# Stick-breaking attention with keys in rising order and factors applied after the value product; retention values projected 512 columns at a time

## The chip, the cores and the metric

The kernel runs on one core of one Trainium2 chip. TensorE is called PE here (its weight loads are PEld), VectorE is DVE, ScalarE is ACT, GpSimd is POOL, and SP issues most of the DMAs. The metric is the device time of one execution in microseconds (us); several runs of each kernel are compared by their median. About 0.2%, some 6 us, is what a measurement of this kernel can tell from no change.

## The reference, cut to what matters

Two layers of a decoder on 1024 tokens of width 1024. The change touches two places: the stick-breaking attention of layer 0 (8 heads of 64, causal without the diagonal), and the value projection of the retention of layer 1 (4 heads, 512 value columns each).

```python
def block(args):                                   # one block of 128 queries, all keys
    z = jnp.einsum('bhqd,bhkd->bhqk', q_i, k) * scale
    mask = kpos[None, :] < qpos[:, None]
    log_fail = jnp.where(mask, jax.nn.log_sigmoid(-z), 0.0)
    later = lax.cumsum(log_fail, axis=3, reverse=True) - log_fail
    a = jnp.where(mask, jnp.exp(jax.nn.log_sigmoid(z) + later), 0.0)
    return jnp.einsum('bhqk,bhkd->bhqd', a, v)
...
proj = h @ w_in                                    # retention: rq, rk, rv, rg are column ranges of proj
```

So the weight of key s for query t is exp(z_ts - softplus(z_ts) - the sum of softplus(z_tj) over the keys j between s and t).

## The kernel before, in words

Large products are made of float32r operands split into a high and a low part: three matmuls hi·hi, lo·hi, hi·lo per 128 rows of the contraction (`mm3`, L182 to L185). Weights come from HBM in units of 128x1024 by `w_pump`: SP loads `raw`, ACT casts `whi` (L168), DVE subtracts `wlo` (L169); three units at most are in flight.

**Stick-breaking (L849 to L1018)** works on scores laid out with keys on the partitions and queries along the free dimension. A *step* is one block of 128 keys against 256 queries of two heads, so its tiles are 128x512. There are 80 steps: 20 for each of four pairs of heads p, and within a pair two chains of query blocks are interleaved, i = 3 then 0 in one and i = 2 then 1 in the other. Query block i has 2i+2 key blocks. Of the 20 steps of a pair, 4 have kb = 2i+1, where only the last 128 queries of each head count (c0 = 128): these *diagonal* steps have 128x256 tiles, and the other 16 *full* steps have 128x512.

The engines run this part in the order in which the code is written (`manual_schedule`). In iteration n the loop goes through a list of tokens `SORDER`, each the stage of a step with an offset from n:

```python
SORDER = "Z+3 V-4 f Q+0 A+3 W+0 K+3 X-1 E+3 p p h+2 L+3 f C-1 l+2 M+3".split()
LSB, ABB, SHB = 8, 4, 3
```

The stages before: Z (PE, L869, L870, and a mask product L872 near the diagonal) writes z into a PSUM bank, of which pool `pz` has two; A, E, L (ACT, L877, L880, L883) make ln(1 + exp(-|z|)) in `ab`; K (DVE, L887) copies z to `ls` in SBUF; M (DVE, L890) makes softplus(z) from `ls` and `ab`; h (DVE, L896) and l (POOL, L899) split it into `sh` and `sl`; Q (PE, L910, L911) adds minus its sum over this block's own keys to a running PSUM bank `Pb` of the chain; W (DVE, L914) adds `Pb` to `ls`; X (ACT, L973) takes the exponential, the attention weight; C (PE, L922, L923) adds to `Pb` the rest of this block, for the next one (not in a chain's last step of a query block); V (PE, L932) multiplies by the values and sums all blocks of one query block in a PSUM bank `av`, which ACT copies to `ob` at the end (L934). The keys go down from the diagonal, so that `Pb` holds all later blocks. An f32 product like V stands in the trace as two instructions.

The token `f` (twice in an iteration) puts other PE work between: until n = 8 the last values' projection of layer 0 (`vps`, L464, four units of 3 matmuls of 256 columns an iteration), and from n = 18 on the first half of the output projection (`ops`, L183 to L185: 64 units of three 128x512 matmuls, spread at about one an iteration). An odd share goes to the first `f`, so a share of one leaves the second `f` empty. From n = 13 to 19 four tiles of `xs` are split there (L988 on ACT, L989 on DVE). The token `p` advances the preparation of the next pair's keys and queries (ACT L525 and L537, POOL L527 and L543), begun at the iterations that `PREPS` lists.

**Retention values (`v_half`, L1479 to L1500)**: for each head and each half of the tokens, 512 tokens times 512 columns with a contraction of 1024. Tokens are the stationary operand and the weights move, 256 columns at a time: 192 matmuls of 128x256, into `rvps`. It runs for heads 0 to 2 of the first half (while `norm_ops` makes the second half's inputs on DVE, ACT and POOL), then for heads 0 to 3 of the second half, and once more (head 3, first half) inside the retention core later.

Of the kernel before, what the change touches and what calls it, by code (L numbers as in the profile page):

```python
# [11 lines left out]
F32R = mybir.dt.float32r  # L12
AF = mybir.ActivationFunctionType
# [48 lines left out]
def tile_trunk(ctx: ExitStack, tc: tile.TileContext, xT, cbc, adaT, vec, w_hyb, w_hout, w_rin, w_rout,  # L62
# [443 lines left out]
    def stack(tag, nm, p, half):  # L506
        i = 2 * p + 1 - half
        return (sqs[0] if i % 3 else sb0).tile([P, HT], F32R, tag=tag, name=nm, bufs=2 if i % 3 else 1)

    def prep_qk(p, isq, half, new, dma=None):  # L510
# [3 lines left out]
        if not isq:  # L514
# [7 lines left out]
            for h in range(2):  # L522
                kh = stacks[p, "kh", h, half] = stack(f"kh{h}", f"kh{p}{h}", p, half)
                kl = stacks[p, "kl", h, half] = stack(f"kl{h}", f"kl{p}{h}", p, half)
                A.copy(kh, xs_[h])  # L525
                yield
                G.tensor_tensor(kl, xs_[h], kh.bitcast(F32), op=ALU.subtract)  # L527
                yield
# [5 lines left out]
        for h in range(2):  # L534
            o = slice(h * 64, h * 64 + 64)
            qs = stacks[p, "q", h, half] = stack(f"q{h}", f"q{p}{h}", p, half)
            A.copy(qs[o], x[o])  # L537
            ts.append(qs)
            yield
# [6 lines left out]
    def s_first():  # L546

        scr = sb0.tile([P, 4, P], F32R, tag="scr", name="scr")
        G.dma_start(scr[:, 0:3, :], cst[:, C_NSTR:C_NSTR + 3, :])
        V.tensor_copy(scr[:, 3, :], ident)  # L550
        scrs.append(scr)
        for isq in range(2):
            for _ in prep_qk(0, isq, 1, half_tile):
                pass
# [294 lines left out]
    with ExitStack() as sx:  # L849
        pz = sx.enter_context(tc.tile_pool(name="pz", bufs=2, space=PSUM))  # L850
        pP = sx.enter_context(tc.tile_pool(name="pP", bufs=1, space=PSUM))
        pav = sx.enter_context(tc.tile_pool(name="pav", bufs=1, space=PSUM))
        steps = []
        for p in range(4):
            two = [[dict(p=p, i=i, kb=kb, x=x, first=(kb == 2 * i + 1), last=(kb == 0), c0=128 if kb == 2 * i + 1 else 0)
                    for i in ii for kb in range(2 * i + 1, -1, -1)] for x, ii in enumerate(((3, 0), (2, 1)))]
            for pair in zip(*two):
                steps.extend(pair)
        cur = {}
        fin = []  # L860
# [13 lines left out]

        def stage_a(s):
            s["ab"] = ab = sp_.tile([P, HT], F32, tag="ab", name="ab", bufs=ABB).rearrange("p (h n) -> p h n", h=2)[:, :, s["c0"]:]
            A.activation(ab, s["z"], AF.Abs)  # L877
# [7 lines left out]
        def stage_k(s):  # L885
            s["ls"] = ls = sp_.tile([P, HT], F32, tag="ls", name="ls", bufs=LSB).rearrange("p (h n) -> p h n", h=2)[:, :, s["c0"]:]
            V.tensor_copy(ls, s["z"])  # L887

        def stage_sp(s):
            V.scalar_tensor_tensor(s["ab"], s["ls"], 0.0, s["ab"], op0=ALU.max, op1=ALU.add)  # L890

        def stage_hi(s):
            c0 = s["c0"]
            s["sh"] = sp_.tile([P, 2, 256], F32R, tag="sh", name="sh", bufs=SHB)[:, :, c0:]
            s["sl"] = sp_.tile([P, 2, 256], F32R, tag="sl", name="sl", bufs=SHB)[:, :, c0:]
# [5 lines left out]
        def stage_h(s):  # L901
            stage_hi(s)
            stage_lo(s)

        def stage_t1(s):
            c0 = s["c0"]
            if s["first"]:
                cur["P", s["x"]] = pP.tile([P, 2, 256], F32, tag=f"P{s['x']}", name="Pb")
            s["P"] = Pc = cur["P", s["x"]][:, :, c0:]
            PE.matmul(Pc, nstr, s["sh"], start=s["first"], stop=False, skip_group_check=True)  # L910
            PE.matmul(Pc, nstr, s["sl"], start=False, stop=True, skip_group_check=True)  # L911

        def stage_t2(s):
            V.tensor_tensor(s["ls"], s["ls"], s["P"], op=ALU.add)  # L914

        def stage_t(s):
            stage_t1(s)
            stage_t2(s)

        def stage_c(s):  # L920
            if not s["last"]:
                PE.matmul(s["P"], ncom, s["sh"], start=False, stop=False, skip_group_check=True)  # L922
                PE.matmul(s["P"], ncom, s["sl"], start=False, stop=True, skip_group_check=True)  # L923

        def stage_av(s):
            p, i, kb, c0 = s["p"], s["i"], s["kb"], s["c0"]
            if s["first"]:
                cur["av", s["x"]] = pav.tile([P, 256], F32, tag=f"av{s['x']}", name="av")
            av = cur["av", s["x"]]
            for h in range(2):  # L930
                o = slice(h * 64, h * 64 + 64)
                PE.matmul(av[o, c0:], vts[p][:, kb, o], s["ls"][:, h, :], start=s["first"], stop=True, skip_group_check=True)  # L932
            if s["last"]:
                fin.append(lambda: A.copy(obt[p][:, i * 256:i * 256 + 256], av))  # L934
# [5 lines left out]
        nstr, ncom, negm, idr = (scrs[0][:, i, :] for i in range(4))  # L940
# [8 lines left out]
        with tc.manual_schedule(engines=COMPUTE):  # L949
# [3 lines left out]
            prep = [prep_qk(0, 0, 0, new_x, QD(nc)), prep_qk(0, 1, 0, new_x, QD(nc))]  # L953
# [18 lines left out]
            def stage_x(s):  # L972
                A.activation(s["ls"], s["ls"], AF.Exp)  # L973
# [843 lines left out]
```

## Time and profile before

| | |
|---|---|
| median of 3 runs | 3144.05 us (3142.46 to 3146.39) |
| profiled execution, its own time | 3141.93 us |
| its span, first to last instruction | 3140.2 us |
| PE busy over the span | 3004.1 us (96%) |
| DVE, ACT, POOL busy | 2142.7, 1247.6, 487.4 us |
| stick-breaking, 619 to 855 us: PE, DVE, ACT, POOL busy | 227.08, 217.59, 196.81, 155.20 of 236.00 us |
| retention values, 1598 to 1767 us: PE, DVE busy | 163.75, 66.38 of 169.00 us |

Start times count from the first instruction. A matmul's row has its start and a modelled length: matmuls are pipelined, so the next one starts before the length is over, and the distance of two starts is what one costs on PE. In a row of groups, the numbers after the bar are the busy time in us, the mean in ns, and the idle time of the engine just before with what ended it. PEclk is the share of the full TensorE clock that was granted.

### The profile page before, as it was taken

What the parts mean: (1) busy time and instruction counts of PE and PEld (TensorE: products, weight loads), DVE (VectorE), ACT (ScalarE), POOL (GpSimd) and SP (SyncE); (2) the same over time, 40 slices, a digit from 0 to 9 for tenths busy, and PEclk for the clock granted to TensorE, in tenths of its full rate; (3) what the DMA queues carried; (4) which work ended last, traced back from release to release, by engine and by line L of the source; (5) the groups of instructions that cost most, each with busy time, mean ns of one, the idle gap of its engine ahead of it and who ended that gap; (6) DMA issues with size and microseconds to landing.
All of it is one profiled execution on the core that took longest, in us unless ns stands there. A gap on an engine that the chain in (4) does not pass through costs nothing.

```text
span 3140.2 us, 39706 instructions
## 1 busy us (share of the span) xinstructions
PE 3004.1 (96%) x15118; PEld 2456.4 (78%) x15118; DVE 2142.7 (68%) x3084; ACT 1247.6 (40%) x2026; POOL 487.4 (16%) x352
## 2 busy tenths in 40 slices
PE   4999999999999999999989999999999899999999
PEld 3787788867677888877879888887778688888887
DVE  8778876599887655588582455578856876556445
ACT  5445456688763222221252332333323632223111
POOL 3233332077430000000030000001111300000000
PEclk9999999999999999999999999999999999999999
DMA  6433332341034322287134333362212342224223
GB/s 214 139 108 104 118 112 79 98 142 45 21 105 150 101 86 87 86 318 263 60 98 138 106 114 110 109 235 106 102 54 62 124 147 88 82 89 156 100 74 101
DMA packets 142640, 363.35 MB, mean 116 GB/s; under 512 B 15216, under 2 KB 31216, under 8 KB 141936
## 3 DMA queue, kind: packets, MB, share of 16 engines
q1 hardware_dynamic: 141840, 359.82, 34.6%
q8 instruction: 119, 1.95, 0.3%
q10 hardware_dynamic: 464, 0.79, 0.1%
q14 instruction: 73, 0.60, 0.1%
q0 software_dynamic: 144, 0.20, 0.0%
HBM read 283.67 MB, written 77.07 MB: 115 GB/s over the span
## 4 chain that ended last, share of the span: by engine, by line
PE 71%; DVE 17%; DMA 4%; ACT 3%; issue 3%; POOL 0%; SPq 0%; DVEq 0%; ACTq 0%; POOLq 0%
PE ops L183 6%; PE ops L184 5%; PE ops L185 5%; PE rvps L1494 4%; PE mB L1218 4%; PE mB L1216 4%; PE mB L1217 4%; PE mD L1218 3%; PE mD L1217 3%; PE mD L1216 3%; PE mA L1216 3%; PE mA L1218 3%; PE mA L1217 3%; PE mE L1216 2%; PE mE L1217 2%
## 5 line engine op out<-in xcount | busy, mean ns | idle before, releaser
L331 DVE SCALAR_TENSOR_TENSOR x<-ops,mod,x 128x512 f32<-128x512 f32 x288 | 215.1, 748 | 216.2 <-PE ops L185 215.4
L168 ACT CAST whi<-raw 128x1024 fp32r<-128x1024 f32 x159 | 166.6, 1050 | 388.1 <-PE ops L184 307.4
L169 DVE TENSOR_TENSOR wlo<-raw,whi 128x1024 fp32r<-128x1024 f32 x159 | 210.5, 1326 | 117.6 <-ACT whi L168 113.1
L183 PE MATMUL ops<-hdh,whi 128*128 128x512 f32 x704 | 276.8, 393 | 7.1 <-DVE x L331 6.5
L184 PE MATMUL ops<-hdl,whi 128*128 128x512 f32 x704 | 274.8, 390 | 0.0
L185 PE MATMUL ops<-hdh,wlo 128*128 128x512 f32 x704 | 274.4, 390 | 0.0
L183 PE MATMUL gps<-hh,whi 128*128 128x512 f32 x352 | 166.1, 472 | 0.0
L183 PEld LDWEIGHTS ops<-hdh,whi 128*128 128x128 f32 x704 | 132.2, 188 | 42.6 <-DVE x L331 13.2
L185 PEld LDWEIGHTS ops<-hdh,wlo 128*128 128x128 f32 x704 | 132.2, 188 | 27.8 <-issue 0.2
L219 POOL TENSOR_TENSOR nscr<-nscr 128x512 f32<-128x512 f32 x30 | 45.9, 1531 | 692.5 <-ACT nscr L218 635.0
L184 PEld LDWEIGHTS ops<-hdl,whi 128*128 128x128 f32 x704 | 132.2, 188 | 27.0 <-issue 0.2
L1208 ACT CAST thi<-raw 128x512 fp32r<-128x512 f32 x180 | 101.7, 618 | 107.7 <-DVE raw L1204 66.0
L184 PE MATMUL gps<-hl,whi 128*128 128x512 f32 x352 | 140.0, 398 | 0.0
L185 PE MATMUL gps<-hh,wlo 128*128 128x512 f32 x352 | 140.0, 398 | 0.0
L183 PE MATMUL ops<-osh,whi 128*128 128x512 f32 x320 | 128.5, 406 | 10.2 <-DVE x L331 8.1
L899 POOL TENSOR_TENSOR sl<-ab,sh 128x512 fp32r<-128x512 f32 (+1 forms) x80 | 116.2, 1452 | 140.6 <-ACT ab L883 73.8
L184 PE MATMUL ops<-osl,whi 128*128 128x512 f32 x320 | 128.1, 401 | 5.2 <-DVE osl L1673 4.7
L185 PE MATMUL ops<-osh,wlo 128*128 128x512 f32 x320 | 126.3, 396 | 0.0
L1209 DVE TENSOR_TENSOR tlo<-raw,thi 128x512 fp32r<-128x512 f32 x180 | 119.1, 708 | 1.6 <-ACT thi L1208 1.6
L1345 ACT ACTIVATE u<-u 128x512 f32<-128x512 f32 x44 | 27.8, 632 | 228.1 <-DVE u L1278 228.1
L1258 DVE TENSOR_TENSOR u<-u,mB 128x512 f32<-128x512 f32 x60 | 41.2, 686 | 110.8 <-issue 97.7
L1278 DVE TENSOR_TENSOR u<-u,mE 128x512 f32<-128x512 f32 x60 | 41.3, 688 | 108.6 <-PE mE L1218 108.6
(400 smaller groups left out, 8725.7 us busy)
## 6 DMA issues: line engine op xcount, KB each, us to landing
raw<-in_w_fin_dram SPq DMA_DIRECT2D x102, 512.0 KB, 3.9
raw<-in_w_rin_dram SPq DMA_DIRECT2D x64, 512.0 KB, 4.2
raw<-in_w_fout_dram SPq DMA_DIRECT2D x52, 512.0 KB, 3.7
adaw<-in_adaT_dram SPq DMA_DIRECT2D x48, 512.0 KB, 5.1
oraw<-hid_d SPq DMA_DIRECT2D x44, 512.0 KB, 5.3
gth<-in_adaT_dram SPq DMA_DIRECT2D x64, 256.0 KB, 2.9
raw<-in_w_hyb_dram SPq DMA_DIRECT2D x29, 512.0 KB, 3.6
hid_d<-c SPq DMA_DIRECT2D x44, 256.0 KB, 2.0
```

Of the source, the lines that this page charges most:

```text
L168: A.copy(hi, raw)
L169: V.tensor_tensor(lo, raw, hi.bitcast(F32), op=ALU.subtract)
L183: PE.matmul(ps, whi, xh, start=start, stop=False)
L184: PE.matmul(ps, whi, xl, start=False, stop=False)
L185: PE.matmul(ps, wlo, xh, start=False, stop=stop)
L331: V.scalar_tensor_tensor(xs[dt][:, sl], ps, gts(dt), xs[dt][:, sl], op0=ALU.mult, op1=ALU.add)
L899: G.tensor_tensor(s["sl"], s["ab"], s["sh"].bitcast(F32), op=ALU.subtract)
L1209: e.tensor_tensor(lo, t, f32(hi), op=ALU.subtract)
L1216: PE.matmul(ps, w[0][:, c], xh[k], start=(start and k == 0), stop=False, skip_group_check=True)
L1217: PE.matmul(ps, w[0][:, c], xl[k], start=False, stop=False, skip_group_check=True)
L1218: PE.matmul(ps, w[1][:, c], xh[k], start=False, stop=(k == 3), skip_group_check=True)
L1494: PE.matmul(ps[:, ti, :], a, b, start=(ti == 0 and k == 0 and n == 0), stop=(k == 7 and n == 2), skip_group_check=True)
```

## The change

Stick-breaking runs the key blocks of a query block in rising order, kb = 0 first and the diagonal last. Q adds minus the block's own sums to z itself, in z's PSUM bank (`pz` now has four), and X takes the exponential from there: K and W (DVE) and the bank `Pb` with C (PE) are gone. What later blocks contribute is applied afterwards: a new S (PE, four matmuls, stationary operand `som`) sums softplus over the block's keys for both heads into the second half of the step's `av` bank; a new G (ACT) takes exp of minus that, a 128x256 tile; V makes the block's value product alone in the first half of the bank; a new R (POOL) multiplies the running output in `ob` by the factor, and a new O (DVE) adds the block's product (copies it in a query block's first step, where S, G and R are absent). The ACT copy of `av` at the end is gone. In full steps A moves from ACT to DVE, as a bitwise and on the bits of z; M reads z from PSUM and no longer `ls`. The order of stages is another, and the preparation follows the new order of keys.

In the retention, `v_rows` takes the place of `v_half` in seven of its eight calls: the weights move 512 columns wide (96 matmuls of 128x512), four token blocks are accumulated at once in four PSUM banks of a pool `pv`, and units of the weights are cut to match. The pool of the product that follows is opened only when it is needed.

```diff
-PREPS = {3: (0, 1), 6: (1, 1), 10: (0, 0), 15: (1, 0)}
-SORDER = "Z+3 V-4 f Q+0 A+3 W+0 K+3 X-1 E+3 p p h+2 L+3 f C-1 l+2 M+3".split()
-LSB, ABB, SHB = 8, 4, 3
+PREPS = {3: (0, 0), 6: (1, 1), 15: (1, 0), 18: (0, 1)}
+SORDER = "O-2 Z+3 E+2 V-1 A+3 f Q+0 S+0 L+2 p X+0 R-1 M+2 G+0 p f h+2 l+2".split()
+WB, ABB, SHB = 3, 4, 3
...
-        pz = sx.enter_context(tc.tile_pool(name="pz", bufs=2, space=PSUM))
-        pP = sx.enter_context(tc.tile_pool(name="pP", bufs=1, space=PSUM))
-        pav = sx.enter_context(tc.tile_pool(name="pav", bufs=1, space=PSUM))
+        pz = sx.enter_context(tc.tile_pool(name="pz", bufs=4, space=PSUM))
+        pav = sx.enter_context(tc.tile_pool(name="pav", bufs=2, space=PSUM))
...
         def stage_a(s):
-            A.activation(ab, s["z"], AF.Abs)
+            if s["c0"]:
+                A.activation(ab, s["z"], AF.Abs)
+            else:
+                V.tensor_scalar(ab.bitcast(I32), s["z"].bitcast(I32), 0x7FFFFFFF, None, op0=ALU.bitwise_and)
...
-        def stage_k(s):
-            V.tensor_copy(ls, s["z"])
         def stage_sp(s):
-            V.scalar_tensor_tensor(s["ab"], s["ls"], 0.0, s["ab"], op0=ALU.max, op1=ALU.add)
+            V.scalar_tensor_tensor(s["ab"], s["z"], 0.0, s["ab"], op0=ALU.max, op1=ALU.add)
...
-            PE.matmul(Pc, nstr, s["sh"], start=s["first"], stop=False, skip_group_check=True)
-            PE.matmul(Pc, nstr, s["sl"], start=False, stop=True, skip_group_check=True)
-        def stage_t2(s):
-            V.tensor_tensor(s["ls"], s["ls"], s["P"], op=ALU.add)
-        def stage_c(s):
-            if not s["last"]:
-                PE.matmul(s["P"], ncom, s["sh"], start=False, stop=False, skip_group_check=True)
-                PE.matmul(s["P"], ncom, s["sl"], start=False, stop=True, skip_group_check=True)
+        def stage_q(s):
+            PE.matmul(s["z"], nstr, s["sh"], start=False, stop=False, skip_group_check=True)
+            PE.matmul(s["z"], nstr, s["sl"], start=False, stop=True, skip_group_check=True)
+        def stage_x(s):
+            A.activation(s["w"], s["z"], AF.Exp)
+        def stage_s(s):
+            s["av"] = av = pav.tile([P, 2, 256], F32, tag="av", name="av")
+            if s["first"]:
+                return
+            for h in range(2):
+                e = som[:, 64 - 64 * h:192 - 64 * h]
+                for j, t in enumerate((s["sh"], s["sl"])):
+                    PE.matmul(av[:, 1, s["c0"]:], e, t[:, h, :], start=(h + j == 0), stop=(h + j == 2), skip_group_check=True)
+        def stage_g(s):
+            if not s["first"]:
+                A.activation(g[:, s["c0"]:], s["av"][:, 1, s["c0"]:], AF.Exp, scale=-1.0)
...
+        def stage_r(s):
+            if not s["first"]:
+                G.tensor_tensor(acc(s), acc(s), s["g"][:, s["c0"]:], op=ALU.mult)
+        def stage_o(s):
+            av = s["av"][:, 0, s["c0"]:]
+            if s["first"]:
+                V.tensor_copy(acc(s), av)
+            else:
+                V.tensor_tensor(acc(s), acc(s), av, op=ALU.add)
...
+    def v_rows(h, half, hi, lo, stage):
+        pss = [pv.tile([P, HT], F32, tag="v", name="rvps") for _ in range(4)]
+        for j in range(4):
+            whi, wlo = (t.rearrange("p (k c) -> p k c", k=2) for t in w_next())
+            for tt in range(4):
+                tk = slice(tt * P, tt * P + P)
+                for i in range(2):
+                    k = 2 * j + i
+                    xh, xl = hi[k][:, tk], lo[k][:, tk]
+                    for n, (a, b) in enumerate(((xh, whi), (xl, whi), (xh, wlo))):
+                        PE.matmul(pss[tt], a, b[:, i, :], start=(k + n == 0), stop=(k + n == 9))
+                if j == 3:
+                    t = stage()
+                    A.copy(t, pss[tt])
+                    nc.sync.dma_start(rv_d[h][:, half * 4 + tt, :], t)
+            yield
```

On PE, in an iteration in the middle of the second pair of heads, before: the end of V, one unit of the output projection, then Q of one step and C of the step before it, and the first matmul of the next Z. `Pb` is the running bank, `z` the score bank, `scr` the constant operands.

```order
L932 MATMUL av_6334<-ls_6119,vt1_5659 64x128
L183 MATMUL ops_6267<-o02_6099,whi_5338 128x512
L184 MATMUL ops_6267<-o12_6100,whi_5338 128x512
L185 MATMUL ops_6267<-o02_6099,wlo_5339 128x512
L910 MATMUL Pb_6216<-sh_6281,scr_4630 128x512 [waits DVE_49]
L911 MATMUL Pb_6216<-sl_6282,scr_4630 128x512 [waits Pool_49]
L922 MATMUL Pb_6242<-sh_6252,scr_4630 128x512 [waits DVE_49]
L923 MATMUL Pb_6242<-sl_6253,scr_4630 128x512
L869 MATMUL z_6361<-q10_5767,kh10_5917 128x256 [waits DVE_49,PE_49]
```

On PE in the same iteration now (`w` is the result of X, `av_6408` the bank of the step whose z is `z_6292`; the fourth matmul of S, which reads as the second, is left out):

```order
L928 MATMUL av_6365<-w_6377,vt1_5654 64x256
L184 MATMUL ops_6327<-o02_6139,whi_5340 128x512
L185 MATMUL ops_6327<-o12_6140,whi_5340 128x512
L186 MATMUL ops_6327<-o02_6139,wlo_5341 128x512
L902 MATMUL z_6292<-sh_6345,scr_4630 128x512
L903 MATMUL z_6292<-sl_6346,scr_4630 128x512 [waits Pool_49]
L917 MATMUL av_6408<-sh_6345,som_5326 128x256 [waits DVE_49]
L917 MATMUL av_6408<-sl_6346,som_5326 128x256
L917 MATMUL av_6408<-sh_6345,som_5326 128x256
L868 MATMUL z_6429<-q10_5781,kh10_6216 128x256 [waits Activation_49]
```

The two products of C became four of S, and the first matmul of the next Z, which waited for DVE, now waits for ACT; so does the V that follows this Z.

On ACT at the same place, before; `ab` is the chain A, E, L of one step, `ls` X of another, `kh` belongs to the preparation:

```order
L877 ACTIVATE ab_6342<-z_6329 128x512 [waits PE_49,Pool_49]
L973 ACTIVATE ls_6222<-ls_6222 128x512 [waits DVE_49]
L880 ACTIVATE ab_6342<-ab_6342 128x512 [waits Activation_49]
L525 CAST kh21_6350<-sx_6312 128x512 [waits DMAHW3_49,DMAHW2_49]
L883 ACTIVATE ab_6342<-ab_6342 128x512 [waits Activation_49]
```

On ACT now; `ab` is E, L of a step two ahead, `w_6415` X and `g_6419` G of the step whose Q stands above:

```order
L526 CAST kh20_6383<-sx_6371 128x512 [waits DMAHW3_49,DMAHW2_49]
L884 ACTIVATE ab_6358<-ab_6358 128x512 [waits DVE_49]
L887 ACTIVATE ab_6358<-ab_6358 128x512 [waits Activation_49]
L907 ACTIVATE w_6415<-z_6292 128x512 [waits PE_49]
L922 ACTIVATE g_6419<-av_6408 128x256 [waits PE_49]
```

X, which followed DVE's W of the iteration before, now follows PE's Q of its own iteration, and reads z's bank. The banks of z are given out in the order `z_6292`, `z_6317`, `z_6350`, `z_6393`, `z_6429`: with four of them, the last takes the place of the first.

More of the change, by code (lines that the diff above doesn't have):

```diff
@@ L933, in stage_av @@
-            if s["last"]:
-                fin.append(lambda: A.copy(obt[p][:, i * 256:i * 256 + 256], av))
+                PE.matmul(s["av"][o, 0, c0:], vts[p][:, kb, o], s["w"][:, h, :], start=True, stop=True, skip_group_check=True)
+        acc = lambda s: obt[s["p"]][:, s["i"] * 256 + s["c0"]:s["i"] * 256 + 256]
+        def stage_r(s):
[7 more added lines that the diff above has]
+                V.tensor_tensor(acc(s), acc(s), av, op=ALU.add)
@@ L939, in tile_trunk @@
         sp_ = sx.enter_context(tc.tile_pool(name="sbp", bufs=2, side="right"))
-        nstr, ncom, negm, idr = (scrs[0][:, i, :] for i in range(4))
+        nstr, negm, idr = (scrs[0][:, i, :] for i in range(3))
+        som = sp_.tile([P, 192], F32R, tag="som", name="som", bufs=1)
+        for i in range(3):
+            V.tensor_scalar(som[:, 64 * i:64 * i + 64], ones[:, 0:64], float(i == 1), None, op0=ALU.mult)
         xs = []
@@ L1167, in wino, with banks @@
     def wino(name, o, fpa, npairs, ne, ev):
-        pf = tc.alloc_tile_pool(name=f"pf{name}", bufs=4, space=PSUM)
+        pf = []
         fpb = []
+        def banks():
+            if not pf:
+                pf.append(tc.alloc_tile_pool(name=f"pf{name}", bufs=4, space=PSUM))
         pairs = {}
@@ L1281, in early @@
         def early(norm):
+            banks()
             for n in range(ne):
```

85 lines of the change are left out of this document (34 added, 51 removed).

## Prediction

> **What bounds the kernel now.** I read the page first, then the busy times of stretches, then who waits for whom on PE, and last the order of time on PE and ACT inside single steps. The page:
>
> ```profile
> PE 3004.1 (96%) x15118; PEld 2456.4 (78%) x15118; DVE 2142.7 (68%) x3084; ACT 1247.6 (40%) x2026; POOL 487.4 (16%) x352
> ```
>
> PE is busy nearly always, so a change pays where PE gets less to do or waits less. The stick-breaking part in four stretches (columns: stretch, its length, then busy time and count of PE, PEld, DVE, ACT, POOL, then the granted clock), and the Q matmuls (L910), one a step, in the third:
>
> ```profile
> 627.00:655.00 28.00, 27.56 (x192) 23.16 (x191) 24.86 (x37) 23.82 (x45) 24.26 (x18) 1.00 0.54 168
> 655.00:693.00 38.00, 32.69 (x180) 22.07 (x180) 37.39 (x59) 33.71 (x67) 23.93 (x18) 0.96 0.46 153
> 693.00:849.00 156.00, 154.25 (x863) 111.86 (x862) 147.31 (x242) 130.07 (x252) 104.91 (x73) 1.00 0.12 36
> 849.00:860.00 11.00, 9.06 (x39) 5.91 (x38) 7.30 (x7) 6.20 (x8) 0.00 (x0) 0.84 0.17 48
> 693.00:849.00 156.00, 21.04 (x57) 10.56 (x57) 1.00 0.12 36
> ```
>
> 57 steps take 156 us, 2.74 each. PE waited for hardly anything there; these are all its waits between 692.5 and 849.5 us (total, times, longest):
>
> ```profile
> PE Pb L922 <- DVE ls L914: 1.1, 1, 1.1
> PE z L869 <- DVE ls L887: 0.6, 1, 0.6
> ```
>
> So the long third stretch is bound by PE's own work, although DVE is at 94%. Only the second, where four large splits fall to DVE and no projection fills PE, is DVE's: 37.39 of 38. One full step on PE, from Q to the next Q (start, length, engine, line):
>
> ```profile
> 764.33 0.39 PE L910 MATMUL Pb<-sh,scr 128*128 128x512 f32 x1
> 764.56 0.39 PE L911 MATMUL Pb<-sl,scr 128*128 128x512 f32 x1
> 764.79 0.39 PE L922 MATMUL Pb<-sh,scr 128*128 128x512 f32 x1
> 765.02 0.39 PE L923 MATMUL Pb<-sl,scr 128*128 128x512 f32 x1
> 765.25 0.28 PE L869 MATMUL z<-q,kh 128*128 128x256 f32 x1
> 765.37 0.28 PE L870 MATMUL z<-q,kl 128*128 128x256 f32 x1
> ...
> 765.81 0.65 PE L932 MATMUL av<-ls,vt 128*64 128x256 f32 x4
> 766.39 0.50 PE L183 MATMUL ops<-o,whi 128*128 128x512 f32 x1
> ...
> 767.19 0.39 PE L910 MATMUL Pb<-sh,scr 128*128 128x512 f32 x1
> ```
>
> Q 0.46, C 0.46, Z 0.56, V 0.58, the unit of the projection 0.80: 2.86 us without a hole. A wide matmul costs 0.23, a 256-column one 0.12. With 256 columns in all, Q and C of diagonal steps cost that too:
>
> ```profile
> 745.48 0.28 PE L911 MATMUL Pb<-sl,scr 128*128 128x256 f32 x1
> 745.60 0.28 PE L922 MATMUL Pb<-sh,scr 128*128 128x256 f32 x1
> 745.71 0.29 PE L923 MATMUL Pb<-sl,scr 128*128 128x256 f32 x1
> 745.84 0.28 PE L869 MATMUL z<-q,kh 128*128 128x256 f32 x1
> ```
>
> **The change, part by part. C against S.** On PE, C (two wide matmuls) goes, S (four narrow ones) comes: 0.46 against 0.48 in a full step. The same columns move, so PE gains nothing. In diagonal steps C cost 0.24; S has four matmuls of 128 columns there, at most 0.12 each as the 256-column ones: 0.47. That alone is 12 x 0.02 + 4 x 0.23 = 1.2 us in 20 steps.
>
> **The new wait.** Before, X could be late: Q, W, X and V were spread over four iterations. Now X needs its own Q, and behind S the next PE instruction is a Z that takes over the bank which X is reading; V behind it needs X's result as well. With a share of one the second `f` is empty, so S is all that PE has meanwhile. The round trip PE, ACT, PE is read from these rows (the first pair is A waiting for Z, the second PE waiting for an ACT copy of a PSUM bank):
>
> ```profile
> 748.83 0.28 PE L870 MATMUL z<-q,kl 128*128 128x256 f32 x1
> 749.21 0.60 ACT L877 ACTIVATE ab<-z 128x512 f32<-128x512 f32 x1 [0.29 <-PE z L870]
> 930.09 0.59 ACT L1227 COPY u<-mA 128x512 f32<-128x512 f32 x1
> 930.73 0.19 PEld L1216 LDWEIGHTS mA<-A12h,whi 128*128 128x128 f32 x1 [0.26 <-ACT u L1227]
> 849.40 0.40 PE L911 MATMUL Pb<-sl,scr 128*128 128x512 f32 x1
> 849.84 0.69 DVE L914 TENSOR_TENSOR ls<-ls,Pb 128x512 f32<-128x512 f32 x1 [1.73 <-PE Pb L911]
> ```
>
> The matmul's length runs out, ACT starts 0.10 later (DVE, in the third pair, 0.04 later), works 0.60 on 128x512 from PSUM, and PE goes on 0.05 after that. From the start of Q's second matmul to the next Z: 0.39 + 0.07 + 0.60 + 0.05 = 1.11 us in a full step, the 0.07 being the middle of the two rows. Unhindered PE would be there after 0.23 + 0.48 = 0.71. For a diagonal step ACT's row for 128x256 from PSUM is
>
> ```profile
> L877 ACT ACTIVATE ab<-z 128x256 f32<-128x256 f32 x16 | 6.1, 379 | 4.4 <-PE z L872 4.2 <-POOL sl L899 0.2
> ```
>
> and the trip 0.28 + 0.07 + 0.38 + 0.05 = 0.78. What stands behind that Z on PE, the V, the projection's unit and the next Q, waits with it.
>
> The sum for 20 steps, from Q's second start to the next Z. Before: 16 x 0.23 + 4 x 0.12 + 12 x 0.46 + 4 x 0.24 = 10.6 us. After: 16 x 1.11 + 4 x 0.78 = 20.9; in the four steps without S the wait is just longer. That is 10.3 more in 20 steps and 29.2 in the 57 of the third stretch; the 1.7 us of waits above go: **+27.5 us** (24 to 31 with 0.04 or 0.10 in place of 0.07). Everything else in a step fits into its new 3.2 us: ACT exchanges A (0.60) for a G of half the size, and the DVE and POOL rows are these:
>
> ```profile
> L890 DVE SCALAR_TENSOR_TENSOR ab<-ls,ab 128x512 f32<-128x512 f32 x64 | 58.7, 918 | 1.7 <-ACT ab L883 1.7
> L887 DVE COPY ls<-z 128x512 f32<-128x512 f32 x64 | 43.6, 681 | 1.0 <-ACT ab L877 1.0
> L914 DVE TENSOR_TENSOR ls<-ls,Pb 128x512 f32<-128x512 f32 x64 | 43.5, 680 | 11.7 <-PE Pb L911 11.2
> L914 DVE TENSOR_TENSOR ls<-ls,Pb 128x256 f32<-128x256 f32 x16 | 6.6, 415 | 0.7 <-PE Pb L911 0.4
> L899 POOL TENSOR_TENSOR sl<-ab,sh 128x512 fp32r<-128x512 f32 x64 | 99.9, 1561 | 47.8 <-DVE sh L896 35.8 <-PE Pb L923 3.1 <-PE Pb L910 2.9
> L899 POOL TENSOR_TENSOR sl<-ab,sh 128x256 fp32r<-128x256 f32 x16 | 16.3, 1016 | 92.8 <-ACT ab L883 73.8 <-DVE sh L896 15.3 <-PE ops L185 3.4
> ```
>
> **DVE's relief.** In a full step K and W (0.68 each) go, A (as K) and O (as the 128x256 of L914, 0.42) come, and M, with one operand in PSUM like L914, takes between that row's 0.68 and its own 0.92; I take 0.68. That is 0.5 us less for DVE. It pays only in the second stretch, 13 steps of which nine are full: 4.5 us. But R comes to POOL there, about 1.0 as l's half-size row, which takes POOL from 23.9 to some 35 of 38. **-3 us** (-5 to +1).
>
> The Trainium skill, SBUF — State Buffer, section "Who interferes with whom", has DVE instructions with two SBUF operands exclude GpSimd instructions that read SBUF, and not those with one. The trace agrees: L890 with two has a mean of 918 against 680 for L914 with one. By that rule M costs 0.68, which is the lower bound taken above.
>
> **Beginning and end.** V comes three iterations earlier: its work moves from the end to the beginning, PE being busy at both. The last wait for `ob` shortens, since no `av` copy stands ahead on ACT: **-1 us** (-3 to 0) of the two that PE lost in the fourth stretch. The second small DMA of the constants lies in an earlier part where nothing waits for it: 0.
>
> **Retention values.** First and last starts of the narrow matmuls; the last four of the eight calls run from 1675.0 to 1766.9:
>
> ```profile
> L1494 PE MATMUL rvps<-whi,A x256: 282/283/284, 1676.4 to 1766.9; 128*128 128x256 f32 x128
> L1494 PE MATMUL rvps<-whi,A11h x128: 278/284/387, 1598.8 to 2118.5; 128*128 128x256 f32 x128
> L1494 PE MATMUL rvps<-whi,A21h x128: 282/284/284, 1675.0 to 1765.3; 128*128 128x256 f32 x128
> ```
>
> That is 23.0 us a call, 0.120 a matmul. 96 wide ones at 0.23 are 22.0: -1.0 a call, -7 for seven. The three calls before took 76.2 us, 7 more than three times 23.0; these waits are for DVE and ACT, which have the same casts to do, and may grow or shrink by 4. **-7 us** (-11 to -2).
>
> **Sum.** +27.5 - 3 - 1 - 7 = +16.5 us, on the profiled execution's 3141.9: 3158.4. That execution lies 2.1 under the median of 3144.05, so I forecast **3160 us** for the median; with the ends of the terms 3149 to 3174.
>
> **Rivals.** *The wait is covered (faster).* Place: between S and the next Z. It decides if X is over 0.71 us after Q's second start, in place of 1.11: the end of a matmul's row is modelled, and PSUM might be ready sooner. Then S against C costs 3.3, the 1.7 goes, and -3, -1, -7 remain: -9.4, 3135 us for the median. Against it: X alone takes 0.60, and the row of L877 shows ACT idle until 0.38 after even a narrow matmul's start. 18%.
>
> *POOL becomes the bound.* For 20 steps: 16 x 1.56 + 4 x 1.02 for l, 12 x 1.02 for R and 4 x 0.75 for its diagonal steps (half the columns again; an estimate from l's two rows), and 8 preparations, whose rows are
>
> ```profile
> L543 POOL TENSOR_TENSOR q<-sx,q 64x512 fp32r<-64x512 f32 x14 | 20.5, 1463 | 1.1
> L527 POOL TENSOR_TENSOR kl<-sx,kh 128x512 fp32r<-128x512 f32 x14 | 19.3, 1379 | 1.6 <-ACT kh L525 1.6
> ```
>
> at 1.42: 56 us, against 20 x 2.74 + 10.3 - 0.6 = 64 on PE by my forecast. It is not the bound on average, but two preparations now begin close together, in iterations 15 and 18 of a pair; where the buffers don't cover that, some 1.5 us are lost in each of five places: 3168. 8%.
>
> *The clock drops.* The forecast leaves PE idle 0.4 of 3.2 us, 13%. The nearest row kept its clock with more:
>
> ```profile
> 680.00:690.00 10.00, 7.40 (x42) 5.17 (x43) 10.00 (x17) 7.71 (x15) 4.12 (x4) 1.00 0.66 209
> ```
>
> 26% idle at a clock of 1.00. In the fourth stretch the clock was 0.84 over 11 us, behind a gap of some 2 us: 1.8 us lost. Should the many short gaps bring ten such drops, it would be 3160 + 18 = 3178. 3%. The Trainium skill, TensorE: Matmul & The Clock Gate, section "A second HAM failure mode: psum-queue depth-cycling", says that short PE idling between groups of matmuls, as banks are cycled, can make the clock swing; by that rule the last case would be the likely one, and this row speaks against it.
>
> *The wide matmuls bring nothing* (the first three calls lose in waits what the columns gain): 3167. 5%.
>
> **How the numbers follow.** Forecast 66%, of which 4 come out within 0.2% (6 us) of before; covered wait 18% (15 faster, 3 the same); the three others 16%, all slower. Faster 0.15, same 0.07, slower 0.78. The forecast's own range is 3149 to 3174; to leave out no more than 2 in 10 it is drawn down to the upper half of the covered case, 3136, and ends at 3172.
>
> **What would show it.** Right: in the changed profile PE waits at Z (L868) for ACT's w (L907) some 50 times, 0.3 to 0.5 each, Q to Q is 3.2 us in full steps, and the third stretch takes some 183 us. Wrong: steps of 2.9 without that wait; or L935 on POOL, or L942 on DVE, as what S and Q wait for; PEclk under 1.0 in these slices. For the retention, seven calls at 22 us each; waits for wlo in the first three above 7 us would be the miss there.

## The result and the profile after

The changed kernel takes 3172.78 us in the median of four runs (3169.27 to 3177.82), the kernel before 3143.26 in the four beside them: a ratio of 1.0095 with a 95% interval of 1.0075 to 1.0115, so 24 to 36 us slower. The forecast was 3160, its range ended at 3172. The profiled execution took 3169.77 us, its span is 3168.0.

The page's busy times of the changed kernel:

```profile
PE 3012.9 (95%) x14574; PEld 2429.6 (77%) x14574; DVE 2105.9 (66%) x3071; ACT 1232.2 (39%) x2010; POOL 510.6 (16%) x417
```

PE's busy time has hardly grown, 3004.1 to 3012.9, while the span grew by 28 us: the time is in waits. The stretches that answer to those shown of before (stretch, length, busy time and count of PE, PEld, DVE, ACT, POOL, granted clock, DMA share, GB/s):

```profile
627.00:657.00 30.00, 29.78 (x213) 24.25 (x212) 18.41 (x33) 21.30 (x42) 25.43 (x24) 1.00 0.53 157
657.00:701.00 44.00, 36.06 (x194) 24.41 (x193) 32.82 (x57) 31.07 (x61) 27.12 (x27) 0.88 0.45 145
701.00:888.00 187.00, 170.48 (x966) 121.18 (x965) 123.21 (x230) 119.35 (x246) 116.41 (x119) 1.00 0.09 28
888.00:899.00 11.00, 8.01 (x39) 5.88 (x38) 6.81 (x7) 5.50 (x7) 0.46 (x1) 1.00 0.15 48
```

The third stretch holds the same 57 steps in 187 us, in place of 156, and PE, which was busy for all but 1.75 us of it, now stands still for 16.5. The second takes 44 instead of 38, and DVE's relief is plain there (32.8 of 44 busy, 37.4 of 38 before), yet it bought nothing; the clock has fallen to 0.88. What PE waited for between 618 and 900 us (total, times, longest), its four largest:

```profile
PE z L868 <- ACT w L907: 18.3, 53, 0.8
PE av L917 <- DVE ob L940: 2.1, 1, 2.1
PE ops L184 <- ACT osh L1452: 1.8, 1, 1.8
PE av L917 <- DVE ob L942: 1.7, 1, 1.7
```

The first row is the wait that the prediction named, 53 times and 0.35 us each. The second and the fourth, S waiting for O on DVE, it had among its signs of being wrong (L942), but at no price. One full step of the third stretch on PE, with X on ACT:

```profile
790.91 0.39 PE L902 MATMUL z<-sh,scr 128*128 128x512 f32 x1
791.14 0.39 PE L903 MATMUL z<-sl,scr 128*128 128x512 f32 x1
791.38 0.28 PE L917 MATMUL av<-sh,som 128*128 128x256 f32 x1
...
791.58 0.60 ACT L907 ACTIVATE w<-z 128x512 f32<-128x512 f32 x1 [1.87 <-PE z L903]
...
791.73 0.28 PE L917 MATMUL av<-sl,som 128*128 128x256 f32 x1
...
792.23 0.39 PE L868 MATMUL z<-q,kh 128*128 128x256 f32 x1 [0.21 <-ACT w L907]
...
792.45 0.28 PE L869 MATMUL z<-q,kl 128*128 128x256 f32 x1
792.57 0.27 PE L868 MATMUL z<-q,kh 128*128 128x256 f32 x1
...
792.89 0.65 PE L928 MATMUL av<-w,vt 128*64 128x256 f32 x4
...
793.47 0.50 PE L184 MATMUL ops<-o,whi 128*128 128x512 f32 x1
...
794.27 0.39 PE L902 MATMUL z<-sh,scr 128*128 128x512 f32 x1
```

S is issued by 791.73, and PE's next instruction, Z at 792.23, stands behind X. From Q's second start to Z it is 1.09 us. The step takes 3.36: 0.23 for Q, 1.09, then 0.66 to V, 0.58 to the unit and 0.80 to the next Q. Each of these is as forecast, within 0.02, but one: Z took 0.56 before and takes 0.66 here, because the first matmul after the wait has its successor 0.22 us behind it and not 0.12.

Where the time came from, stretch by stretch, out of the starts of the matmuls in each kernel's one profile. I runs from the first Z to the Q of step 9 (steps counted from 0), II to the Q of step 22, III to the Q of step 79; "end" from there to the first `mA`, the next product; "values" from the first to the last start of the seven retention calls. The rows below before and after are the experiments that follow; times are medians (the kernel before had 3141.4 to 3142.6 beside the experiments).

| kernel | time, us | I | II | III | end | values |
|---|---|---|---|---|---|---|
| before | 3143.26 | 35.5 | 38.3 | 156.4 | 59.0 | 168.2 |
| after | 3172.78 | 38.4 | 43.9 | 187.3 | 56.8 | 156.9 |
| unit behind S | 3143.96 | 37.9 | 44.0 | 164.3 | 57.1 | 158.5 |
| retention alone | 3129.20 | 35.5 | 38.3 | 156.4 | 57.5 | 159.0 |
| split behind O | 3165.49 | 38.4 | 39.2 | 187.3 | 58.6 | 157.5 |
| X in halves | 3174.90 | 38.6 | 48.4 | 190.6 | 56.8 | 157.4 |
| unit and split | 3142.66 | 37.6 | 37.7 | 165.5 | 57.1 | 157.6 |
| V between S and Z | 3138.55 | 37.2 | 37.2 | 166.0 | 56.7 | 157.4 |
| the same, R on DVE | 3140.18 | 37.2 | 38.0 | 165.0 | 56.7 | 158.4 |
| retention, split late | 3123.71 | 35.5 | 35.8 | 156.6 | 57.5 | 157.3 |
| unit and split, low k on DVE | 3139.31 | 37.7 | 37.7 | 163.4 | 59.3 | 157.0 |

After against before that is +2.9, +5.6, +30.9, -2.2 and -11.3, together +25.9 of the 27.8 by which the two profiled spans differ. Nearly all the rest, 2.2 us, lies between `mA` and the first retention matmul, where the programs are the same up to the units of the weights; the profiles of this table differ there by up to 5.6 us from each other. The runs of one kernel also lie up to 6 us below and 11 above their median, so differences of a few us between kernels are read from these stretches and not from the times.

### The profile page after: what moved, and what is told of

The parts are those of the page before. It is cut to its first block, busy times and chain, and to the rows that moved or that the text cites. A ratio compares the mean times of both kernels' runs of the same rounds, so it can differ in the third digit from the quotient of the medians.

```text
span 3168.0 us, 38538 instructions
## 1 busy us (share of the span) xinstructions
PE 3012.9 (95%) x14574; PEld 2429.6 (77%) x14574; DVE 2105.9 (66%) x3071; ACT 1232.2 (39%) x2010; POOL 510.6 (16%) x417
## 5 line engine op out<-in xcount | busy, mean ns | idle before, releaser
L170 DVE TENSOR_TENSOR wlo<-raw,whi 128x1024 fp32r<-128x1024 f32 x159 | 203.8, 1284 | 104.3 <-ACT whi L169 99.5
L898 POOL TENSOR_TENSOR sl<-ab,sh 128x512 fp32r<-128x512 f32 (+1 forms) x80 | 93.9, 1174 | 158.4 <-ACT ab L887 74.2
L1356 ACT ACTIVATE u<-u 128x512 f32<-128x512 f32 x44 | 27.8, 632 | 231.8 <-DVE u L1287 231.8
```

Of the source, the lines that this page charges most:

```text
L170: V.tensor_tensor(lo, raw, hi.bitcast(F32), op=ALU.subtract)
L898: G.tensor_tensor(s["sl"], s["ab"], s["sh"].bitcast(F32), op=ALU.subtract)
```

## The experiments

**The unit of the projection between S and Z.** Token `f` moves behind S; nothing else.

```diff
-SORDER = "O-2 Z+3 E+2 V-1 A+3 f Q+0 S+0 L+2 p X+0 R-1 M+2 G+0 p f h+2 l+2".split()
+SORDER = "O-2 Z+3 E+2 V-1 A+3 Q+0 S+0 f L+2 p X+0 R-1 M+2 G+0 p f h+2 l+2".split()
```

> The projection's unit (f) is moved from ahead of Q to behind S, so that PE has 0.80 us more of its own work between Q and the next Z. Theory 1, the round trip Q, X, Z bounds the full step: the wait of Z for w disappears, since 0.23 + 0.48 + 0.80 = 1.51 us now pass where 1.11 are needed; a full step takes the sum of PE's own work, 0.46 + 0.48 + 0.80 + 0.56 + 0.58 = 2.88 us instead of 3.37, the third stretch (57 steps) 160 us instead of 187, and the time falls by some 27 us to 3146. The first and second stretch stay as they are. Theory 2, GpSimd (l and R) or another engine bounds the step: the wait changes its name, steps stay above 3.2 us and the time above 3165.

It took 3143.96 us (ratio to before 1.0008, 0.9999 to 1.0017), 29 us less than the changed kernel, and the third stretch 164.3. PE's waits in that stretch:

```profile
PE av L917 <- DVE ob L942: 2.0, 4, 0.6
PE z L868 <- ACT w L907: 0.6, 3, 0.2
PE av L917 <- DVE ob L940: 0.2, 1, 0.2
```

14 us of waiting for w have become 0.6. Of the 27 us between the two profiles the third stretch gives 23, where Theory 1 had 27; most of the rest lies where the two programs are the same, 3.6 of it ahead of the first Z, so that the time came out at 3144 for 3146 is in part luck. A step without holes on PE, from S to the Z behind it and on to Q:

```profile
758.39 0.28 PE L917 MATMUL av<-sl,som 128*128 128x256 f32 x1
758.51 0.39 PE L184 MATMUL ops<-o,whi 128*128 128x512 f32 x1
...
759.20 0.28 PE L868 MATMUL z<-q,kh 128*128 128x256 f32 x1
759.32 0.28 PE L869 MATMUL z<-q,kl 128*128 128x256 f32 x1
...
759.77 0.65 PE L928 MATMUL av<-w,vt 128*64 128x256 f32 x4
760.35 0.50 PE L902 MATMUL z<-sh,scr 128*128 128x512 f32 x1
```

Z waits for nothing, its second matmul is 0.12 behind the first, and Z is back at 0.57. So the round trip is the cause of the third stretch's loss: the same work in another order gives back 23 of its 31 us, and no engine's load was touched. Stretch II, which has no unit to move until step 18, stays at 44.0.

**The retention alone.** The kernel before, with `v_rows` and its units of weights from the changed kernel.

```diff
-        for _ in v_half(h, 0, both("A11", "A12", 0), both("A11", "A12", 1), stage):
+        for _ in v_rows(h, 0, both("A11", "A12", 0), both("A11", "A12", 1), stage):
```

> The kernel before with only the retention values made 512 wide. Theory 1, the retention's gain is its own: its calls end 11 us earlier relative to their start, as in the changed kernel, so 3132. Theory 2, the part of the gain above the 7 us of saved columns came only because the changed kernel reached the retention 39 us later, with its weights already there: 3136. Theory 3, the waits for the weight casts eat it: 3140 or more.

3129.20 us, a ratio of 0.9961 (0.9947 to 0.9976): faster than both kernels. The seven calls take 159.0 us, 9.2 less than before; in the nine other kernels with this edit they take 156.9 to 158.5, which is 9.7 to 11.3 less wherever they begin (157.3 in the run that begins them earliest, the last experiment), so Theory 2 falls. The other 4 of the 13 us lie ahead of these calls, where the profiles differ by as much from each other. The last four calls and the first three, from the rows of the changed kernel:

```profile
L1526 PE MATMUL rvps<-wlo,A x64: 389/389/390, 1719.2 to 1794.6; 128*128 128x512 f32 x64
L1526 PE MATMUL rvps<-whi,A21h x64: 389/389/390, 1707.8 to 1783.3; 128*128 128x512 f32 x64
L1526 PE MATMUL rvps<-whi,A11h x48: 389/389/501, 1637.8 to 1696.3; 128*128 128x512 f32 x48
```

From 1707.8 to 1794.6 and one matmul more are 87.0 us, 21.75 a call or 0.227 a matmul. The first three took 70.0, 4.7 above three times that; before they were 7.2 above.

**DVE's part of the splits behind O.** In stretch II, S waited for O once for 2.1 us. The place in the changed kernel, on PE, DVE and ACT:

```profile
672.45 0.50 PE L902 MATMUL z<-sh,scr 128*128 128x512 f32 x1
...
672.78 0.39 PE L903 MATMUL z<-sl,scr 128*128 128x512 f32 x1
672.82 2.10 DVE L999 TENSOR_TENSOR o<-x,o 128x1024 fp32r<-128x1024 f32 x1 [0.40 <-ACT o L998]
...
674.85 0.41 DVE L940 COPY ob<-av 128x256 f32<-128x256 f32 x1
...
675.31 0.58 PE L917 MATMUL av<-sh,som 128*128 128x256 f32 x1 [2.14 <-DVE ob L940]
675.69 0.42 PE L917 MATMUL av<-sl,som 128*128 128x256 f32 x1
```

S of step n takes over the `av` bank of step n-2, which O of step n-2 must have read. O is the iteration's first token, but the split stands ahead of it on DVE, and it waits for its own cast on ACT. Windows of 2 us around it, and where the clock came back (columns as in the stretches above):

```profile
672.00:674.00 2.00, 1.17 (x8) 0.50 (x7) 1.60 (x2) 2.00 (x4) 1.44 (x2) 1.00 0.00 0
674.00:676.00 2.00, 0.69 (x3) 0.69 (x4) 1.90 (x4) 0.59 (x2) 1.24 (x1) 0.56 0.11 12
676.00:678.00 2.00, 2.00 (x11) 1.81 (x12) 0.58 (x2) 1.40 (x4) 1.44 (x2) 0.50 0.77 250
...
684.00:686.00 2.00, 2.00 (x14) 1.35 (x13) 1.75 (x5) 1.76 (x4) 0.89 (x2) 0.88 0.74 219
```

The clock stood at half until about 684.5. The edit leaves the cast where it was and issues the subtraction, with the DMA that follows it, behind O:

```diff
-SORDER = "O-2 Z+3 E+2 V-1 A+3 f Q+0 S+0 L+2 p X+0 R-1 M+2 G+0 p f h+2 l+2".split()
+SORDER = "O-2 s Z+3 E+2 V-1 A+3 f Q+0 S+0 L+2 p X+0 R-1 M+2 G+0 p f h+2 l+2".split()
...
                         A.copy(oh, xs[4 + k])
-                        V.tensor_tensor(ol, xs[4 + k], oh.bitcast(F32), op=ALU.subtract)
-                        nc.sync.dma_start(xs[4 + k], xT[:, 4 + k, :])
-                        og.append((oh, ol))
+                        splits.append((k, oh, ol))
...
+                    if tok == "s":
+                        for k, oh, ol in splits:
+                            V.tensor_tensor(ol, xs[4 + k], oh.bitcast(F32), op=ALU.subtract)
+                            nc.sync.dma_start(xs[4 + k], xT[:, 4 + k, :])
+                            og.append((oh, ol))
+                        splits.clear()
```

> The changed kernel, but DVE's part of the four large splits (o, 128x1024) is issued behind the accumulation O of the iteration instead of ahead of it. Theory 1, in the second stretch S waits for a bank of av that O frees late because it stands behind such a split on DVE, and the clock halves behind the gap: both waits for ob (2.1 and 1.7 us) and the 10 us at half clock (some 5 us lost) go, 3164 to 3166. Theory 2, the second stretch is bound by ACT (four casts of 1.04 us each ahead of its exponentials) or by DVE's sum: within 2 us of the changed kernel's 3172.8.

3165.49 us (ratio 1.0077, 1.0062 to 1.0092), 7.3 less than the changed kernel, the number of Theory 1. Stretch II takes 39.2, and the windows are these, of the stretch and of the place where the hole had been:

```profile
657.00:696.00 39.00, 32.57 (x191) 22.38 (x191) 33.78 (x53) 30.90 (x62) 28.46 (x26) 1.00 0.49 151
672.00:675.00 3.00, 2.16 (x15) 1.29 (x13) 2.81 (x5) 2.98 (x9) 2.02 (x3) 1.00 0.21 37
675.00:685.00 10.00, 8.02 (x47) 5.57 (x47) 9.20 (x14) 8.78 (x17) 8.84 (x8) 1.00 0.33 91
```

No hole of 2 us, no half clock, and the waits for `ob` fell from 3.8 us to 0.5; those for w rose from 4.0 to 6.0. The stretches show 4.7 of the 7.3 us; the others are within the spread of runs, so that the time met the expectation is in part luck. The edit moved four instructions on DVE's queue and took no work away. How much of the 4.7 is the hole and how much the clock behind it was not separated; in three later runs with the same edit the clock stood at half once in this stretch, for 3.41 us.

**X in two halves.** X as two activations of 128x256.

```diff
-            A.activation(s["w"], s["z"], AF.Exp)
+            for h in range(2):
+                A.activation(s["w"][:, h, :], s["z"][:, h, :], AF.Exp)
```

> The changed kernel, but X is done as two activations of 128x256 (about 0.38 us each, by the rows of w 128x256) instead of one of 128x512 (0.60). Theory 1, the round trip: each full step without other cover becomes 0.17 us longer, in 46 full steps of the third stretch and a few of the second: +8 to +11 us, 3182. Theory 2, something other than X ends the step: no change, 3173.

3174.90 us (ratio to before 1.0107, 1.0090 to 1.0124), 2.1 more than the changed kernel, well short of 8 to 11, and by that number neither theory. The rows say why:

```profile
797.37 0.40 PE L903 MATMUL z<-sl,scr 128*128 128x512 f32 x1
...
797.80 0.66 ACT L908 ACTIVATE w<-z 128x256 f32<-128x256 f32 x2 [0.51 <-PE z L903]
...
798.51 0.33 PE L868 MATMUL z<-q,kh 128*128 128x128 f32 x1 [0.28 <-ACT w L908]
```

Two activations of 0.38 take 0.66 together, since the second starts before the first is over: the dose was 0.06 a step and not 0.17. Q's second start to Z is 1.14 here. 0.06 in each of the 57 steps of stretch III is 3.4 us, and the stretch grew by 3.3. The answer is one to one; the dose was misjudged. Stretch II took 48.4 in this profile because the clock stayed down longer behind the hole (0.64 from 668 to 682, 0.74 from there to 702).

**Both edits, and another cover.** First the unit behind S together with the split behind O.

> The two edits together: the unit behind S and DVE's part of the splits behind O. Theory 1, they act in different stretches (third and second) and add up: 3144.0 - 7.3 = 3137. Theory 2, with the unit behind S the second stretch has another bound and the split costs nothing there any more: 3144.

The stretches add up as Theory 1 had it: II 37.7, III 165.5, and the profiled execution took 3137.19. The median of ten runs is 3142.66 (ratio to before 1.0004, 0.9994 to 1.0014), no better than the unit alone; those runs go from 3137 to 3151, and that time is nearer Theory 2: it doesn't settle what the stretches show.

Then the same wait covered by V instead of the unit, with the split behind O:

```diff
-SORDER = "O-2 s Z+3 E+2 V-1 A+3 f Q+0 S+0 L+2 p X+0 R-1 M+2 G+0 p f h+2 l+2".split()
+SORDER = "V-2 Z+3 O-2 s E+2 A+3 f Q+0 S+0 L+2 p X+0 R-1 M+2 G+0 p f h+2 l+2".split()
```

> Another cover for the same wait: the changed kernel with the splits behind O, the unit back ahead of Q, and V taken one step later (V-2), ahead of Z, with O behind it in the same iteration. PE then has 0.23 + 0.48 + 0.58 = 1.29 us between Q's second matmul and Z, against the 1.11 of the round trip, and that also in the second stretch, where there is no unit to move. Theory 1, the round trip: Z's wait for w is gone in both stretches, the third takes 160 to 165 us and the second 3 to 4 less than the 39.2 of the run with the splits alone, 3133. Theory 2, GpSimd and DVE are next: O and R have one iteration less until S needs the bank, S waits for ob instead of Z for w, and the time stays above 3145.

3138.55 us (ratio 0.9996, 0.9987 to 1.0005). III is 166.0, just above the expected 160 to 165: a second order, which covers the wait with other work, removes 21 us where the first removed 23. In II it gained 2.0 on 39.2, not 3 to 4; PE's waits there:

```profile
PE z L868 <- ACT w L907: 2.3, 3, 1.0
PE av L917 <- DVE ob L940: 1.4, 1, 1.4
PE av L928 <- DVE ob L942: 0.6, 1, 0.6
PE z L903 <- POOL sl L898: 0.4, 1, 0.4
```

A part of the wait for w went over to O and l, which is Theory 2's mechanism. In III, where S waits for `ob` 2.5 us in all, it is as small as with the unit moved (2.2).

**GpSimd.** Two runs took work from it. R on VectorE in the run with V ahead of Z (`G.tensor_tensor` to `V.tensor_tensor` at L935):

> The run with V ahead of Z, with the factor's product R on VectorE instead of GpSimd (128x256, both operands in SBUF). Theory 1, GpSimd isn't a bound: no gain, 0 to +5 us against that run. Theory 2, R on GpSimd is what O and so S wait for: the waits for ob shrink, 3 to 8 us less.

3140.18 us (ratio 1.0000, 0.9987 to 1.0012), III 165.0 for 166.0, II 38.0 for 37.2: no gain. And the low parts of k (L528, likewise) in the run with the unit and the split:

> The run with the unit behind S and the split behind O (third stretch 165.5 us), with the low parts of k in the preparations (L528, 128x512, 1.3 us each, four a pair) on VectorE instead of GpSimd. Theory 1, with the round trip covered, GpSimd in the iterations with preparations delays R, O and so the bank that S waits for: the steps of 3.2 there become 2.9, the third stretch 162. Theory 2, GpSimd is no bound there either: 165 to 167.

3139.31 us (ratio 0.9988, 0.9979 to 0.9997), III 163.4 for 165.5: 2 us, between the two expectations. GpSimd is not what bounds either stretch; at the preparations it costs a little.

**A version that beats both.** The kernel before with the wide retention, and its splits moved in the same manner, behind K (token `s` after `K+3`).

> A try for a version better than both: the kernel before with the 512-wide retention values, and DVE's part of the four large splits issued behind K instead of at the head of the iteration, so that W, which C and X wait for, is ahead of it. Theory 1, in the second stretch the kernel before also loses where a split stands ahead of what PE waits for (its waits for ls, some 4 us, and 6 us at a clock of 0.7): the stretch of 38.3 us shortens by 2 to 4 us, 3126. Theory 2, DVE's sum bounds that stretch (37.4 of 38 us busy), and the order doesn't matter: 3129, as the run with the retention alone.

3123.71 us in five runs (3121.40 to 3124.81), a ratio of 0.9940 (0.9928 to 0.9953): 18 us faster than before and 49 faster than the changed kernel. Stretch II fell from 38.3 to 35.8. Windows of stretches II and III, and the four splits in the kernel before (L989) and here (L1005), with their busy time in us and their mean in ns:

```profile
650.00:686.00 36.00, 32.13 (x182) 22.44 (x181) 35.42 (x59) 33.69 (x67) 23.51 (x17) 0.95 0.49 166
686.00:843.00 157.00, 155.32 (x868) 112.16 (x866) 148.14 (x244) 130.22 (x253) 105.42 (x73) 1.00 0.12 36
L989 DVE TENSOR_TENSOR o<-x,o 128x1024 fp32r<-128x1024 f32 x4 | 8.1, 2026 | 0.0
L1005 DVE TENSOR_TENSOR o<-x,o 128x1024 fp32r<-128x1024 f32 x4 | 5.4, 1353 | 0.0
```

PE's waits at C for `ls` are gone, as Theory 1 had it. But DVE is as full as it was, 35.4 of 36 us for 37.4 of 38, so its busy time fell by about as much as the stretch: the four splits took 8.1 us before and 5.4 here. Before, each of them began while GpSimd was in an l, and they took 1.75 to 2.31; here two run with GpSimd idle, and these take 1.21. So Theory 2's bound, DVE's sum, is not refuted: the new place made the sum itself smaller. Which of the two gave the 2.5 us was not separated. The clock did not: it stood at half for 3.41 us in this stretch in both kernels.

## Why the prediction missed

The direction and the main mechanism were right: slower, by a new wait of Z for X with only S between. The size was not, 3160 against 3172.8; between the profiled spans it is +27.8 for the +16.5 of the sum, 11.3 short. By its steps:

- **The new wait**, +27.5 forecast, +30.9 measured. The trip of 1.11 us was right (1.09). By the prediction's own terms a full step takes 2.86 - 0.69 + 1.11 = 3.28 us (its 3.2 is the mean with the diagonal steps), and it took 3.36: the term left out is PE's restart, 0.10 us behind each wait. The third stretch has 44 of the 53 waits, so 4.4 us, and the trip's 0.02 less gives 0.9 of it back: about the 3.4 that were missed. The bounds were a slip: 0.04 or 0.10 in place of 0.07 moves 57 steps by 1.7 us, which makes 26 to 29 and not 24 to 31. That the trip is the cause is shown twice, by the unit and by V in its place; its answer to a dose, by X in halves.
- **DVE's relief**, the step that failed: "It pays only in the second stretch" and -3 us, against +5.6, so 8.6 of the 11.3. The relief itself came (32.8 us busy for 37.4), and DVE's sum may well have bounded the stretch before. What failed is the step from less work to less time: it did not ask what bounds the stretch once DVE has room. O comes first in the iteration and the split ahead of it, and with two `av` banks S waits for that O, 3.8 us in two waits; behind the first the clock was at half for 10 us. With the split behind O, 4.7 of the 5.6 us were gone. And the round trip, which the prediction counted in the third stretch alone, binds in the second too: 4.0 of the 18.3 us of waits for w lie in it, where no unit helps, and 6.0 once the splits are out of the way. With both covered, by V ahead of Z, the stretch takes 37.2, 1.1 less than before.
- **Beginning and end**, -1 forecast: +2.9 in I and -2.2 at the end. V's work did move from the one to the other (12 instructions of 0.145, 1.7 us, ahead of step 9); the sum is +0.7.
- **Retention**, -7 forecast, -11.3 measured, 9 to 11 in the other kernels. A wide matmul costs 0.227 and was taken at 0.23, from two starts of two decimals: 192 x 0.120 against 96 x 0.227 is 1.25 a call, 8.7 for seven. The waits in the first three calls shrank by another 2.5 instead of staying.
- **S against C**, close to the forecast: a full step whose work lies without holes takes 2.88 us in the run with the unit moved, 2.86 before. All S of the third stretch take 22.3 us there, from start to start, where all C took 19.9 before; most of that difference lies in the diagonal steps, where the prediction had it.
- **The rivals.** The covered wait is out. GpSimd as the bound: out, though the low parts of k cost 2 us at the preparations. The clock: it stayed at 1.00 through 187 us in which PE stood still in nearly every step, as the prediction argued, and fell in II, from where the prediction had taken its row that kept 1.00 (its table has 0.96 for that stretch before). That the wide matmuls bring nothing is out: alone they give 0.4%.

What stays open: with the wait covered, III takes 163 to 166 us, 7 to 10 more than before. In the run with the unit moved it is 7.9, and PE's matmuls, counted from start to start, divide it: 2.4 for S in place of C, 1.0 for eight more mask products (in the new order other steps fall into the stretch), and 4.5 more for holes ahead of S and Z, of which the profile lists 2.8 as waits for `ob` and w. Taking R or the low k from GpSimd moved the stretch by 1 and 2 us. A single cause of the holes wasn't found.

## What to carry to other kernels

When a stage moves from a bank that nobody needs soon to one that the next instruction on PE takes over, write down the round trip in us and the work that PE has meanwhile; if the trip is longer, move independent work between, or an order that is otherwise good loses in every step. An engine's busy share in a stretch does not say that less work there saves time: look at which instruction stands ahead of the one that frees a bank, since a long optional one is better issued behind it. Part of a busy time can also be another engine's doing: the same four splits took 8.1 us in one place and 5.4 in another. When a change joins two independent edits, time them apart: here the one gained 0.4% by itself, and so the other lost some 1.3% (1.0095 over 0.9961). Even in the best order tried the new attention takes 3139 us with the wide retention, and the old takes 3129.

## What the runs showed of the hardware

- **One hole of 2.14 us put PE's clock at half for ten.** The last matmul ahead of the hole ends at 673.17 (672.78 and 0.39). The window from 674 to 676 shows 0.56, so the clock fell at about 674.2, 1.1 us into the hole; the one from 684 to 686 shows 0.88, so it was back at about 684.5. In the run with the split behind O, with 2.16 of 3 us busy at the same place, it stayed at 1.00. A rule by the length of a hole alone doesn't come out of this: the second hole of the same trace, 1.66 us from 690.25 to 691.90, left the clock at 1.00:

```profile
690.00:693.00 3.00, 1.34 (x11) 1.02 (x9) 3.00 (x4) 1.36 (x5) 3.00 (x3) 1.00 0.31 124
```

The traces record each change of the clock. Between 610 and 910 us every stay at half, in all eleven, lasts 3.41 us or three times that (674.23 to 684.47 here; 668.24 to 671.65 and 855.98 to 859.39 in the kernel before), and the changes within one trace lie whole multiples of 3.41 apart. So it may matter where a hole lies on that grid. Which stretches of it bring the clock down is not shown. The Trainium skill, TensorE: Matmul & The Clock Gate, section "Why this matters for your kernels", warns of idle gaps over about 3 us. Here one of 2.14 was enough, and the measurement decides.
- **Many short waits don't.** The third stretch kept 1.00 with 44 waits of a third of a us. The Trainium skill, TensorE: Matmul & The Clock Gate, section "A second HAM failure mode: psum-queue depth-cycling", has short idling between groups of matmuls make the clock swing. That is not borne out here.
- **PE restarts 0.10 late.** Behind a wait the second narrow matmul starts 0.22 after the first, without one 0.12. It is not the wait alone: behind V, where the rows show no wait of PE, the second wide matmul of the unit starts 0.34 after the first (793.47 and 793.81), the third 0.23 after that.
- **Two activations in a row overlap.** Two of 0.38 took 0.66. The Trainium skill, ScalarE: Activation LUTs, section "What ACT_TABLE_LOAD costs", gives an overlap of some 93 ns back to back. The trace agrees, 0.10.
- **DVE and GpSimd hold each other up when DVE reads two operands from SBUF.** With M's z in PSUM and K and W gone, l and M take less than before:

```profile
L898 POOL TENSOR_TENSOR sl<-ab,sh 128x512 fp32r<-128x512 f32 x64 | 82.2, 1284 | 148.7 <-ACT ab L887 74.2 <-DVE sh L895 51.1 <-PE z L903 11.6
L891 DVE SCALAR_TENSOR_TENSOR ab<-z,ab 128x512 f32<-128x512 f32 x64 | 43.9, 686 | 20.8 <-ACT ab L887 20.7
```

l's mean fell from 1561 to 1284 ns and M's from 918 to 686. The 918 is a mean of two kinds: before, 15 of the 64 M's began while GpSimd was in an instruction and took 1.33 to 1.79 us, and the other 49 took 0.68 to 0.69. Now 40 begin so, and none takes over 0.69. It goes the other way too: behind the split of 672.82, whose operands are both in SBUF, a half-size R took 1.44 us (673.80), where another took 0.46 (692.61). This agrees with the section of the Trainium skill that the prediction drew on, SBUF — State Buffer, "Who interferes with whom".
